# A decoder trunk's last layer: expert rows added to the output in DRAM instead of turned back into tokens

## Chip, cores and metric

The kernel runs on one core of a Trainium2 chip. The time is the device time of one execution in microseconds, as the median of the runs of a kernel. The engines are named as the profile names them: PE for matrix products (PEld is its weight load, which runs beside the products), DVE for vectors, ACT for activations, POOL for GpSimd, SP for the queue that starts most DMAs.

## The reference

A trunk of two layers over 256 tokens of width 1024, all in float32. Layer 0 is attention and a dense SwiGLU, layer 1 a gated recurrence and a layer of 8 experts, of which each token uses 2. Only the last part is touched here:

```python
logits = (t @ w_router).astype(F32)
top_vals, top_idx = lax.top_k(logits, TOP_K)
top_w = jax.nn.softmax(top_vals, axis=-1)
gates = jnp.sum(jax.nn.one_hot(top_idx, N_EXPERTS, dtype=F32) * top_w[..., None], axis=1)
out = jnp.zeros((B * S, D), F32)
for e in range(N_EXPERTS):
    y = swiglu(t, w_gate[e], w_up[e], w_down[e]).astype(F32)
    out = out + gates[:, e:e + 1] * y
```

The output is the residual `h` plus `out`. An expert's three matrices are 1024 x 3584, 1024 x 3584 and 3584 x 1024 floats, 44 MB together; all eight are read once, 352 MB.

## The kernel before

**Precision.** A product of float32 quality is made of three passes in a faster format: a weight is split into `w_hi` (ACT copies and rounds, L91) and `w_lo` (DVE subtracts, L91), rows likewise, and `mm3` (L100 to L103) issues high x high, high x low and low x high. A split covers 128 x 1024 weights and feeds six products of 128 x 128 by 512 columns. Split buffers are four deep (`NSUB`), buffers of raw weights fourteen deep (`NRAW`), 1 MB each; SP starts a load when a raw buffer comes free.

**Routing and slots.** `route` finds each token's two experts (`sel`), their weights (`gw`) and each token's slot in its expert's 128 rows (`place`, by products with a triangle of ones and a block of ones, L1034 to L1037). `one_hot` compares `place` with the slot numbers, and `gather_pair` multiplies the tokens' rows (`nh`, `nl`) by that 0/1 matrix: 32 products of 256 columns bring the rows of two experts into slots at once. Experts thus come in pairs: 0 and 1, 2 and 3, and so on.

**Jobs.** An expert's 3584 hidden columns are seven chunks of 512; a chunk is a `Job` with `gate`, `up`, `turn` (four transposes of the 128 x 512 hidden block, then `hh` on ACT and `hl` on DVE, one buffer each) and `down`, which accumulates in two banks `py` over all seven chunks. A job has twelve splits, that is 72 products, and reads 6.3 MB. `run_jobs` weaves them: gate of this job, turn of the one before, up, down of the one before. Before experts 2, 4 and 6 a job is `fresh`: the pair is gathered first, then the previous job is turned and finished. Which instruction really comes next on an engine's queue is settled at build time by the framework, which lets later work go ahead where it takes an engine for idle; the queue itself then runs strictly in order.

**Leaving the slots.** When an expert's last chunk is down, `back_to_tokens` transposes its two 0/1 blocks, and `scatter` takes `py` apart into a high and a low part (ACT and DVE, for each half of the columns), multiplies each by `back` (for two halves and two blocks of tokens, two products each: eight of 512 columns) and lets DVE add the result times the gate into `h` (L1204, four times). The last job does this half by half and sends `h` to the output with `put`, so the output is written once, at the very end.

**More than 128 tokens.** After all jobs a count of each expert's tokens is made (L1254 to L1261). Every engine loads the largest into a register and branches around a second pass that is needed only if some expert has more than 128 tokens. With these inputs it is skipped.

Of the kernel before, what the change touches and what calls it, by code (L numbers as in the profile page):

```python
# [39 lines left out]
def tile_trunk(  # L40
# [935 lines left out]
    mc = ctx.enter_context(tc.tile_pool(name="mc", bufs=1))  # L976

# [6 lines left out]
    _, _, rx, pw = norm_T(hg_, gain_m, acc, into=dense)  # L984

# [5 lines left out]
    nc.vector.tensor_scalar(ei, slot1[:, 0:NE], -1.0, None, op0=ALU.add)  # L991
    up = moe.tile([P, P], F32, name="up", tag="hm", bufs=1)
# [12 lines left out]
    sel = mc.tile([P, NT, NE], F32, name="sel")  # L1005
    gw = mc.tile([P, NT, NE], F32, name="gw")
    place = mc.tile([P, NT, NE], F32, name="place")

    def route():
# [10 lines left out]
        for t in range(NT):  # L1020
# [12 lines left out]

            pp = bank("tp")  # L1034
            for u in range(t + 1):
                nc.tensor.matmul(pp[:, 0:NE], lhsT=up if u == t else ones, rhs=sel[:, u], start=(u == 0), stop=(u == t))
            nc.vector.scalar_tensor_tensor(place[:, t], pp[:, 0:NE], 1.0, sel[:, t], op0=ALU.add, op1=ALU.mult)  # L1037
# [22 lines left out]
    def gather_pair(oneh):  # L1060
# [17 lines left out]
    NCH = FE // 512  # L1078

    class Job:  # L1080

        def __init__(self, ch, shared, es, weights, oneh, gates, fresh=None):
            self.ch, self.shared, self.es, self.oneh, self.gates, self.fresh = ch, shared, es, oneh, gates, fresh
# [39 lines left out]
        def down(self):  # L1123
# [10 lines left out]
            if ch == NCH - 1:  # L1134
                back = back_to_tokens(self.oneh(sh))
                for c in range(2):
                    scatter(c, sh["py"][c], back, self.gates(sh))

    class LastJob(Job):

        def down(self):
            sh = self.shared
            back = back_to_tokens(self.oneh(sh))
            for c in range(2):
# [5 lines left out]
                scatter(c, sh["py"][c], back, self.gates(sh), put)  # L1150

    class FirstJob(Job):
# [16 lines left out]
        def up(self):  # L1169
            sh = self.shared  # L1170
            sh["oneh"] = one_hot(0)
            sh["xg"] = gather_pair(sh["oneh"])
            pt = bank("tp")
# [8 lines left out]
    def back_to_tokens(oneh):  # L1182
        pt = bank("tp")
        for t in range(NT):
            nc.tensor.transpose(out=pt[:, t * P:(t + 1) * P], in_=f32(oneh[t]), identity=ident)
        back = moe.tile([P, S], F32R, name="back", tag="back", bufs=1)
        nc.scalar.activation(back, pt[:, 0:S], AF.Copy)
        return back

    def scatter(c, py, back, gate, done=None):  # L1190

        if c == 0:
            y = lows.tile([P, 2, 512], F32R, name="y", tag="low1")
            yh, yl = y[:, 0], y[:, 1]
        else:
            yh = moe.tile([P, 512], F32R, name="yh", tag="hh", bufs=1)
            yl = moe.tile([P, 512], F32R, name="yl", tag="hl", bufs=1)
        nc.scalar.activation(yh, py, AF.Copy)
        nc.vector.tensor_sub(yl, py, f32(yh))
        for t in range(NT):  # L1200
            ps = bank("tp")
            nc.tensor.matmul(ps, lhsT=back[:, TOK[t]], rhs=yh, start=True, stop=False)
            nc.tensor.matmul(ps, lhsT=back[:, TOK[t]], rhs=yl, start=False, stop=True)
            nc.vector.scalar_tensor_tensor(h[t][:, HALF[c]], ps, gate[t], h[t][:, HALF[c]], op0=ALU.mult, op1=ALU.add)  # L1204
            if done:
                done(t, c)
# [22 lines left out]
    for e in range(NE):  # L1229
        if e % 2 == 0:  # L1230
            shared = {}

            def fresh(sh, e=e):
                sh["oneh"] = one_hot(e)
                sh["xg"] = gather_pair(sh["oneh"])
# [4 lines left out]
        def oneh(sh, e=e):  # L1240
            return [sh["oneh"][:, t, e % 2, :] for t in range(NT)]

        def gates(sh, e=e):
            return [gw[:, t, e:e + 1] for t in range(NT)]

        for ch in range(NCH):
            kind = {(0, 0): FirstJob, (NE - 1, NCH - 1): LastJob}.get((e, ch), Job)
            jobs.append(kind(
                ch, shared, slice((e % 2) * P, (e % 2 + 1) * P), (moe_w_gate[0, e], moe_w_up[0, e], moe_w_down[0, e]), oneh, gates,
# [86 lines left out]
```

## Time and profile before

| what | value |
|---|---|
| median of 3 runs | 1505.01 us (1504.41 to 1505.1) |
| the profiled execution | 1505.47 us, its span 1503.8 us |
| TensorE clock granted, mean | 0.997 of full speed |
| PE, PEld busy | 98%, 82% |
| DVE, ACT, POOL busy | 83%, 69%, 1% |
| moved by DMA | 429.85 MB, 427.41 MB of it read from HBM |

The span runs from the first instruction to the last, and the execution takes some 1.7 us more around it. The layer of experts fills the span from about 490 us on. Matrix products are pipelined, so that the bars of two neighbours overlap: a busy PE tells that it has work, and the distance from one product's start to the next tells its pace.

### The profile page before, as it was taken

The numbers are of one execution on the slowest core, as the hardware profiler recorded it, in microseconds if no ns is written. First come the engines' busy times: TensorE is split into PE (matmuls) and PEld (weight loads), VectorE is DVE, ScalarE is ACT, GpSimd is POOL, SyncE is SP. The second block draws the span as 40 slices with busy tenths as digits, with TensorE's granted clock in tenths as the row PEclk, the third lists the DMA queues.
The fourth block names the chain that finished last, engine by engine and source line by source line (L and its number), as shares of the span: only waits on it lengthen the run. The fifth ranks groups of instructions, "written<-read, shape, count | busy, mean of one in ns | idle before, by whom it ended". The sixth has DMA issues, their size and how long they took to land.

```text
span 1503.8 us, 20241 instructions
## 1 busy us (share of the span) xinstructions
PE 1469.5 (98%) x7573; PEld 1226.1 (82%) x7573; DVE 1243.1 (83%) x1474; ACT 1042.0 (69%) x1293; POOL 14.9 (1%) x32
## 2 busy tenths in 40 slices
PE   7999999999999999999999999999999999999997
PEld 6886899998898788888888878888877888877885
DVE  7785655566777899999999998898889889889886
ACT  6655544445666788878778877777777777777774
POOL 1000000000000000000000000000000000000000
PEclk9999999999999999999999999999999999999999
DMA  9933455655454499999999999989999998999970
GB/s 310 368 122 112 152 175 193 187 180 180 141 168 141 159 369 376 373 357 378 326 340 385 368 339 359 358 325 362 358 365 345 370 357 319 363 362 346 365 253 31
DMA packets 208683, 429.85 MB, mean 286 GB/s; under 512 B 7290, under 2 KB 58530, under 8 KB 208578
## 3 DMA queue, kind: packets, MB, share of 16 engines
q1 hardware_dynamic: 208082, 426.82, 79.8%
q0 software_dynamic: 496, 1.67, 0.4%
q8 instruction: 61, 1.00, 0.3%
q14 instruction: 44, 0.36, 0.1%
HBM read 427.41 MB, written 1.05 MB: 285 GB/s over the span
## 4 chain that ended last, share of the span: by engine, by line
PE 91%; DVE 4%; ACT 2%; issue 1%; DMA 1%; POOL 0%; SPq 0%; ACTq 0%; DVEq 0%; POOLq 0%
PE acc L102 17%; PE acc L101 17%; PE acc L103 16%; PE pj L103 8%; PE pj L102 8%; PE pj L101 8%; PE pj L342 3%; PE pj L343 3%; PE pj L344 3%; DVE w_lo L91 2%; PE tp L1116 1%; PE pj L760 1%; PE pj L761 1%; PE pj L762 1%; ACT w_hi L91 1%
## 5 line engine op out<-in xcount | busy, mean ns | idle before, releaser
L91 DVE TENSOR_TENSOR w_lo<-raw,w_hi 128x1024 fp32r<-128x1024 f32 x810 | 958.5, 1221 | 155.0 <-ACT w_hi L91 137.8
L91 ACT ACTIVATE w_hi<-raw 128x1024 fp32r<-128x1024 f32 x810 | 835.9, 1058 | 271.1 <-PE acc L103 97.5
L102 PE MATMUL acc<-w_lo,xgh 128*128 128x512 f32 x904 | 357.1, 395 | 0.9
L101 PE MATMUL acc<-w_hi,xgh 128*128 128x512 f32 x904 | 355.8, 394 | 1.0 <-ACT xgh L294 1.0
L103 PE MATMUL acc<-w_hi,xgl 128*128 128x512 f32 x904 | 353.2, 391 | 0.0
L102 PEld LDWEIGHTS acc<-w_lo,xgh 128*128 128x128 f32 x904 | 169.7, 188 | 50.4 <-DVE w_lo L91 14.4
L101 PEld LDWEIGHTS acc<-w_hi,xgh 128*128 128x128 f32 x904 | 169.7, 188 | 36.3 <-ACT xgh L294 1.2
L103 PEld LDWEIGHTS acc<-w_hi,xgl 128*128 128x128 f32 x904 | 169.8, 188 | 33.9
L102 PE MATMUL pj<-w_lo,hh 128*128 128x512 f32 x448 | 177.1, 395 | 0.3
L103 PE MATMUL pj<-w_hi,hl 128*128 128x512 f32 x448 | 174.6, 391 | 0.3
L101 PE MATMUL pj<-w_hi,hh 128*128 128x512 f32 x448 | 161.1, 391 | 2.2 <-ACT hh L1120 1.7
L101 PEld LDWEIGHTS pj<-w_hi,hh 128*128 128x128 f32 x448 | 84.1, 188 | 21.5 <-ACT hh L1120 2.7
L102 PEld LDWEIGHTS pj<-w_lo,hh 128*128 128x128 f32 x448 | 84.2, 188 | 18.1 <-DVE w_lo L91 1.6
L103 PEld LDWEIGHTS pj<-w_hi,hl 128*128 128x128 f32 x448 | 84.0, 188 | 17.5 <-DVE hl L1121 1.1
L342 PE MATMUL pj<-xh,w_hi 128*128 128x256 f32 x320 | 90.8, 284 | 0.6 <-DVE hm L677 0.6
L343 PE MATMUL pj<-xl,w_hi 128*128 128x256 f32 x320 | 90.5, 283 | 0.0
L344 PE MATMUL pj<-xh,w_lo 128*128 128x256 f32 x320 | 90.5, 283 | 0.0
L1106 ACT ACTIVATE sg<-acc 128x512 f32<-128x512 f32 x55 | 33.0, 599 | 46.7 <-PE acc L103 46.7
L342 PEld LDWEIGHTS pj<-xh,w_hi 128*128 128x128 f32 x320 | 61.4, 192 | 1.2 <-DVE hm L677 0.8
L343 PEld LDWEIGHTS pj<-xl,w_hi 128*128 128x128 f32 x320 | 61.4, 192 | 0.4
L344 PEld LDWEIGHTS pj<-xh,w_lo 128*128 128x128 f32 x320 | 61.4, 192 | 0.0
L1120 ACT ACTIVATE hh<-tp 128x512 fp32r<-128x512 f32 x56 | 33.3, 595 | 40.4 <-PE pj L102 33.2
(296 smaller groups left out, 1637.1 us busy)
## 6 DMA issues: line engine op xcount, KB each, us to landing
raw<-in_moe_w_gate_dram SPq DMA_DIRECT2D x112, 1024.0 KB, 6.5
raw<-in_moe_w_up_dram SPq DMA_DIRECT2D x112, 1024.0 KB, 7.2
raw<-in_moe_w_down_dram SPq DMA_DIRECT2D x110, 1024.0 KB, 7.0
raw<-in_ffn_w_gate_dram SPq DMA_DIRECT2D x22, 512.0 KB, 3.8
raw<-in_ffn_w_up_dram SPq DMA_DIRECT2D x22, 512.0 KB, 4.8
raw<-in_ffn_w_down_dram SPq DMA_DIRECT2D x11, 1024.0 KB, 4.8
raw<-in_hgrn_w_in_dram SPq DMA_DIRECT2D x10, 1024.0 KB, 5.8
raw<-in_attn_w_in_dram SPq DMA_DIRECT2D x16, 512.0 KB, 9.3
```

What stands on the lines that cost most here:

```text
L91: split.last = nc.scalar.activation(hi, view, AF.Copy), nc.vector.tensor_sub(lo, view, f32(hi))
L101: nc.tensor.matmul(ps, lhsT=xh, rhs=wh, start=first, stop=False, skip_group_check=chk)
L102: nc.tensor.matmul(ps, lhsT=xh, rhs=wl, start=False, stop=False, skip_group_check=chk)
L103: nc.tensor.matmul(ps, lhsT=xl, rhs=wh, start=False, stop=last, skip_group_check=chk)
L342: nc.tensor.matmul(o, lhsT=wh[:, i, j], rhs=xh[:, k], start=k == 0 and j == 0, stop=False, skip_group_check=True)
L343: nc.tensor.matmul(o, lhsT=wh[:, i, j], rhs=xl[:, k], start=False, stop=False, skip_group_check=True)
L344: nc.tensor.matmul(o, lhsT=wl[:, i, j], rhs=xh[:, k], start=False, stop=k == KT - 1, skip_group_check=True)
L760: nc.tensor.matmul(o, lhsT=wh[:, k], rhs=xh[:, k], start=first, stop=False, skip_group_check=True)
L761: nc.tensor.matmul(o, lhsT=wh[:, k], rhs=xl[:, k], start=False, stop=False, skip_group_check=True)
L762: nc.tensor.matmul(o, lhsT=wl[:, k], rhs=xh[:, k], start=False, stop=last, skip_group_check=True)
L1106: nc.scalar.activation(self.sg, ps, AF.Silu)
L1120: nc.scalar.activation(self.hh, ptv, AF.Copy)
```

## The change

The residual `h` is written to the output before the experts start. From then on an expert's rows are added to the output in DRAM: ACT scales `py` by the slot's gate into a tile `y`, and POOL starts an indirect DMA that adds each of the 128 slot rows (4 KB) to the row of the output that an index names. `back_to_tokens` and `scatter` go. So that no slot is without a token, `place` is now a permutation of all 256 tokens for each expert, the chosen ones first, the others behind with a gate of 0. Token number and gate (in two parts) stand in `info`, and `slot_rows` brings them into slot order with four small products per pair.

The two scalings of an expert (`scaled`) wait in a list `later` and are placed on ACT behind the second and third split of the following gate. At a fresh pair the previous job's `turn` moves from behind the gather into its middle (`between`). The last job adds each half of the columns by its own DMA. The count now comes out of `route`. Small tiles get a pool `bits`.

```diff
+    for t in range(NT):
+        nc.gpsimd.dma_start(out=out[0, TOK[t], :], in_=h[t])
+    out_rows = out[0]
+    out_halves = out[0].rearrange("t (c d) -> (t c) d", c=2)
...
     def route():
...
-            pp = bank("tp")
-            for u in range(t + 1):
-                nc.tensor.matmul(pp[:, 0:NE], lhsT=up if u == t else ones, rhs=sel[:, u], start=(u == 0), stop=(u == t))
-            nc.vector.scalar_tensor_tensor(place[:, t], pp[:, 0:NE], 1.0, sel[:, t], op0=ALU.add, op1=ALU.mult)
...
+        pp = bank("tp")
+        for u in range(NT):
+            nc.tensor.matmul(pp[:, 0:NE], lhsT=ones, rhs=sel[:, u], start=(u == 0), stop=(u == NT - 1), skip_group_check=True)
+        for t in range(NT):
+            for u in range(t + 1):
+                nc.tensor.matmul(pp[:, (t + 1) * NE:(t + 2) * NE], lhsT=up if u == t else ones, rhs=sel[:, u], start=(u == 0),
+                                 stop=(u == t), skip_group_check=True)
+        nc.vector.tensor_copy(count, pp[:, 0:NE])
+        for t in range(NT):
+            before = pp[:, (t + 1) * NE:(t + 2) * NE]
+            u = bits.tile([P, 2, NE], F32, name="u", tag="u")
+            nc.vector.scalar_tensor_tensor(u[:, 0], before, 2.0, count, op0=ALU.mult, op1=ALU.subtract)
+            nc.vector.scalar_tensor_tensor(u[:, 0], u[:, 0], ntok[:, t:t + 1], sel[:, t], op0=ALU.add, op1=ALU.mult)
+            nc.vector.scalar_tensor_tensor(u[:, 1], before, -1.0, count, op0=ALU.mult, op1=ALU.add)
+            nc.vector.scalar_tensor_tensor(place[:, t], u[:, 1], tok[:, t:t + 1], u[:, 0], op0=ALU.add, op1=ALU.add)
+        nc.vector.tensor_scalar(place, place, 1.0, None, op0=ALU.add)
+        nc.vector.tensor_copy(info[:, :, :, 1], gw)
+        nc.vector.tensor_sub(info[:, :, :, 2], gw, f32(info[:, :, :, 1]))
...
+    def slot_rows(lhs, rhs, n):
+
+        ps = bank("tp")
+        for j in range(n):
+            for t in range(NT):
+                nc.tensor.matmul(ps[:, 4 * j:4 * j + 4], lhsT=lhs(t, j), rhs=rhs(t, j), start=(t == 0), stop=(t == NT - 1),
+                                 skip_group_check=True)
+        v = bits.tile([P, n, 4], F32, name="sv", tag=f"sv{n}")
+        nc.vector.tensor_copy(v, ps[:, 0:4 * n].rearrange("p (j c) -> p j c", c=4))
+        gate = bits.tile([P, n], F32, name="gate", tag=f"gate{n}")
+        nc.vector.tensor_add(gate, v[:, :, 1], v[:, :, 2])
+        idx = bits.tile([P, 3, n], I32, name="idx", tag=f"idx{n}")
+        nc.vector.tensor_copy(idx[:, 0], v[:, :, 0])
+        for c in range(2):
+            nc.vector.tensor_scalar(idx[:, 1 + c], v[:, :, 0], 2.0, float(c), op0=ALU.mult, op1=ALU.add)
+        return gate, idx
...
+    def gather_pair(oneh, between=None):
 
         xg = slot_tiles(2 * P)
         for k0 in range(0, KT, 2):
+            if k0 == 4 and between:
+                between()
...
     def into(self, w):
...
+                    if later and k0 + i:
+                        with tc.issue_after(split.last[0].ins):
+                            later.pop(0)()
...
     def down(self):
...
             if ch == NCH - 1:
-                back = back_to_tokens(self.oneh(sh))
-                for c in range(2):
-                    scatter(c, sh["py"][c], back, self.gates(sh))
+                later.extend(self.add(0, 2, out_rows, 0))
+
+        def add(self, c0, c1, rows, i):
+
+            (gate, idx), j, py = self.shared["slots"], self.slot, self.shared["py"]
+            box = {}
+
+            def scaled(c):
+                if c == c0:
+                    box["y"] = lows.tile([P, 2, 512], F32, name="y", tag="low1")
+                nc.scalar.activation(box["y"][:, c], py[c], AF.Copy, scale=gate[:, j:j + 1])
+                if c == c1 - 1:
+                    out_of(box["y"])
+
+            def out_of(y):
+                nc.gpsimd.indirect_dma_start(
+                    out=rows, out_offset=bass.IndirectOffsetOnAxis(ap=idx[:, i, j:j + 1], axis=0),
+                    in_=y[:, c0:c1].rearrange("p a b -> p (a b)"), in_offset=None, bounds_check=rows.shape[0] - 1,
+                    oob_is_err=True, compute_op=ALU.add)
+
+            return [lambda c=c: scaled(c) for c in range(c0, c1)]
 
     class LastJob(Job):
...
-            back = back_to_tokens(self.oneh(sh))
             for c in range(2):
...
-                scatter(c, sh["py"][c], back, self.gates(sh), put)
+                for step in self.add(c, c + 1, out_halves, 1 + c):
+                    step()
...
             if job and job.fresh:
-                job.fresh(job.shared)
-                if prev:
-                    prev.turn()
-                    prev.down()
-                    prev = None
+                job.fresh(job.shared, prev.turn)
+                prev.down()
+                prev = None
...
-    pc_ = bank("tp")
-    nc.tensor.matmul(pc_[:, 0:NE], lhsT=ones, rhs=sel[:, 0], start=True, stop=False)
-    nc.tensor.matmul(pc_[:, 0:NE], lhsT=ones, rhs=sel[:, 1], start=False, stop=True)
     cmax = mc.tile([P, 1], F32, name="cmax")
-    nc.vector.tensor_reduce(out=cmax, in_=pc_[:, 0:NE], axis=AX.X, op=ALU.max)
+    nc.vector.tensor_reduce(out=cmax, in_=count, axis=AX.X, op=ALU.max)
```

The second pass and its loop get the same treatment; it is not executed here.

## Rows read from the trace of the kernel before

**Rows 1.** The page: the chain that ended last, and the two groups of splits.

```profile
PE 91%; DVE 4%; ACT 2%; issue 1%; DMA 1%; POOL 0%; SPq 0%; ACTq 0%; DVEq 0%; POOLq 0%
...
L91 DVE TENSOR_TENSOR w_lo<-raw,w_hi 128x1024 fp32r<-128x1024 f32 x810 | 958.5, 1221 | 155.0 <-ACT w_hi L91 137.8
L91 ACT ACTIVATE w_hi<-raw 128x1024 fp32r<-128x1024 f32 x810 | 835.9, 1058 | 271.1 <-PE acc L103 97.5
```

**Rows 2.** Waits from 620 to 1480 us: waiter, releaser, total us, times, longest.

```profile
ACT w_hi L91 <- PE acc L103: 45.1, 151, 1.2
...
PEld acc L102 <- DVE w_lo L91: 14.4, 36, 0.6
```

**Rows 3.** Waits of SP's queue over the span, same columns.

```profile
SPq L85 <- DVE w_lo L91: 1173.8, 381, 17.2
```

**Rows 4.** Windows, 550 to 600 us: engines' busy us, clock, DMA share, GB/s.

```profile
550.00:600.00 50.00, 50.00 (x228) 41.40 (x227) 46.45 (x42) 40.73 (x42) 0.00 (x0) 1.00 1.01 376
```

**Rows 5.** DMA issues: count, KB each, median us to landing.

```profile
raw<-in_moe_w_gate_dram SPq DMA_DIRECT2D x112, 1024.0 KB, 6.5
...
out_dram<-h SPq DMA_DIRECT2D x4, 256.0 KB, 2.1
```

**Rows 6.** Timeline of ACT: the gates' activations, and two of `hh`.

```profile
523.14 0.60 ACT L1106 ACTIVATE sg<-acc 128x512 f32<-128x512 f32 x1 [0.31 <-PE acc L103]
...
623.99 0.60 ACT L1106 ACTIVATE sg<-acc 128x512 f32<-128x512 f32 x1 [0.30 <-PE acc L103]
624.49 0.59 ACT L1120 ACTIVATE hh<-tp 128x512 fp32r<-128x512 f32 x1
...
643.06 0.60 ACT L1106 ACTIVATE sg<-acc 128x512 f32<-128x512 f32 x1 [0.31 <-PE acc L103]
...
659.83 0.60 ACT L1106 ACTIVATE sg<-acc 128x512 f32<-128x512 f32 x1 [0.30 <-PE acc L103]
...
727.04 0.60 ACT L1106 ACTIVATE sg<-acc 128x512 f32<-128x512 f32 x1 [0.30 <-PE acc L103]
...
767.47 0.60 ACT L1106 ACTIVATE sg<-acc 128x512 f32<-128x512 f32 x1 [0.30 <-PE acc L103]
...
1310.59 0.60 ACT L1120 ACTIVATE hh<-tp 128x512 fp32r<-128x512 f32 x1 [1.45 <-PE pj L102]
...
1333.38 0.60 ACT L1106 ACTIVATE sg<-acc 128x512 f32<-128x512 f32 x1 [1.30 <-PE acc L103]
...
1350.50 0.60 ACT L1106 ACTIVATE sg<-acc 128x512 f32<-128x512 f32 x1 [1.30 <-PE acc L103]
...
1422.54 0.60 ACT L1106 ACTIVATE sg<-acc 128x512 f32<-128x512 f32 x1 [1.31 <-PE acc L103]
...
1473.84 0.60 ACT L1106 ACTIVATE sg<-acc 128x512 f32<-128x512 f32 x1 [1.30 <-PE acc L103]
```

**Rows 7.** Timeline of PE at the change from expert 1 to 2.

```profile
743.32 0.50 PE L101 MATMUL pj<-w_hi,hh 128*128 128x512 f32 x1 [0.47 <-ACT hh L1120]
```

**Rows 8.** The end: timeline from 1484 us, and line 1262's branch on PE.

```profile
1489.93 0.60 ACT L1198 ACTIVATE y<-pj 128x512 fp32r<-128x512 f32 x1 [1.93 <-PE pj L103]
...
1493.03 0.39 PE L103 MATMUL pj<-w_hi,hl 128*128 128x512 f32 x1
...
L1262 PEldq COMPARE_BRANCH  x1: 4448/4448/4448, 1498.2 to 1498.2; - x1
```

**Rows 9.** Timelines of POOL, DVE and PE at the start of the experts.

```profile
488.73 0.96 POOL L997 DMA_DIRECT2D gT<-in_moe_w_router_dram  x1
...
488.85 0.69 DVE L310 TENSOR_TENSOR hg<-h,gain 128x512 f32<-128x512 f32 x1
...
491.33 0.68 DVE L310 TENSOR_TENSOR hg<-h,gain 128x512 f32<-128x512 f32 x1
...
504.90 0.17 DVE L1037 SCALAR_TENSOR_TENSOR place<-tp,sel 128x8 f32<-128x8 f32 x1 [0.69 <-PE tp L1036]
...
506.42 0.63 PE L1069 MATMUL acc<-oneh,nh 128*128 128x256 f32 x4
```

More of the change, by code (lines that the diff above doesn't have):

```diff
@@ L976, in tile_trunk @@
     mc = ctx.enter_context(tc.tile_pool(name="mc", bufs=1))
+    bits = ctx.enter_context(tc.tile_pool(name="bits", bufs=2))
     def slot_tiles(n):
@@ L991, in tile_trunk @@
     nc.vector.tensor_scalar(ei, slot1[:, 0:NE], -1.0, None, op0=ALU.add)
+    ti = bits.tile([P, NT], I32, name="ti", tag="ti", bufs=1)
+    nc.gpsimd.iota(ti, pattern=[[P, NT]], base=0, channel_multiplier=1)
+    tok = mc.tile([P, NT], F32, name="tok")
+    nc.vector.tensor_copy(tok, ti)
+    ntok = mc.tile([P, NT], F32, name="ntok")
+    nc.vector.tensor_scalar(ntok, tok, -1.0, None, op0=ALU.mult)
     up = moe.tile([P, P], F32, name="up", tag="hm", bufs=1)
@@ L1005, in tile_trunk @@
     sel = mc.tile([P, NT, NE], F32, name="sel")
+    zero = mc.tile([P, NT * NE], F32, name="zero")
+    nc.gpsimd.memset(zero, 0.0)
     gw = mc.tile([P, NT, NE], F32, name="gw")
     place = mc.tile([P, NT, NE], F32, name="place")
+    count = mc.tile([P, NE], F32, name="count")
+    info = mc.tile([P, NT, NE, 4], F32R, name="info")
+    nc.vector.tensor_copy(info[:, :, :, 3], zero[:, 0:NT * NE].rearrange("p (t e) -> p t e", e=NE))
+    nc.vector.tensor_copy(info[:, :, :, 0], tok[:, :, None].to_broadcast([P, NT, NE]))
     def route():
@@ L1058, in one_hot, with pair_rows @@
         return oneh
-    def gather_pair(oneh):
+    def slot_rows(lhs, rhs, n):
[13 more added lines that the diff above has]
+        return gate, idx
+    def pair_rows(oneh, e):
+        return slot_rows(lambda t, j: oneh[:, t, j], lambda t, j: info[:, t, e + j], 2)
+    def gather_pair(oneh, between=None):
         xg = slot_tiles(2 * P)
         for k0 in range(0, KT, 2):
+            if k0 == 4 and between:
+                between()
             for src, dst in ((nh, xg[0]), (nl, xg[1])):
@@ L1078, in tile_trunk, with __init__ @@
     NCH = FE // 512
+    later = []
     class Job:
-        def __init__(self, ch, shared, es, weights, oneh, gates, fresh=None):
-            self.ch, self.shared, self.es, self.oneh, self.gates, self.fresh = ch, shared, es, oneh, gates, fresh
+        def __init__(self, ch, shared, es, weights, slot, fresh=None):
+            self.ch, self.shared, self.es, self.slot, self.fresh = ch, shared, es, slot, fresh
             self.wg, self.wu = [w.rearrange("(kt p) c -> p kt c", p=P) for w in weights[:2]]
@@ L1172, in up @@
             sh["xg"] = gather_pair(sh["oneh"])
+            sh["slots"] = pair_rows(sh["oneh"], 0)
             pt = bank("tp")
@@ L1180, in up @@
             super().up()
[L1182 to L1206, printed above, removed]
     def run_jobs(jobs):
@@ L1231, in tile_trunk, with fresh @@
             shared = {}
-            def fresh(sh, e=e):
+            def fresh(sh, between, e=e):
                 sh["oneh"] = one_hot(e)
-                sh["xg"] = gather_pair(sh["oneh"])
+                sh["xg"] = gather_pair(sh["oneh"], between)
+                sh["slots"] = pair_rows(sh["oneh"], e)
             if e == 0:
                 route()
[L1240 to L1244, printed above, removed]
         for ch in range(NCH):
@@ L1248, in tile_trunk @@
             jobs.append(kind(
-                ch, shared, slice((e % 2) * P, (e % 2 + 1) * P), (moe_w_gate[0, e], moe_w_up[0, e], moe_w_down[0, e]), oneh, gates,
+                ch, shared, slice((e % 2) * P, (e % 2 + 1) * P), (moe_w_gate[0, e], moe_w_up[0, e], moe_w_down[0, e]), e % 2,
                 fresh if e in (2, 4, 6) and ch == 0 else None))
     run_jobs(jobs)
-    pc_ = bank("tp")
-    nc.tensor.matmul(pc_[:, 0:NE], lhsT=ones, rhs=sel[:, 0], start=True, stop=False)
-    nc.tensor.matmul(pc_[:, 0:NE], lhsT=ones, rhs=sel[:, 1], start=False, stop=True)
     cmax = mc.tile([P, 1], F32, name="cmax")
-    nc.vector.tensor_reduce(out=cmax, in_=pc_[:, 0:NE], axis=AX.X, op=ALU.max)
+    nc.vector.tensor_reduce(out=cmax, in_=count, axis=AX.X, op=ALU.max)
     cmax_i = mc.tile([P, 1], I32, name="cmax_i")
@@ L1269, in tile_trunk @@
             pc = small.tile([P, NT, 2], F32, name="pc", tag="pc")
+            info2 = bits.tile([P, NT, 4], F32R, name="info2", tag="info2")
             oh2 = moe.tile([P, NT, P], F32R, name="oh2", tag="oneh")
@@ L1275, in tile_trunk @@
                 nc.vector.tensor_scalar(oh2[:, t], slot1, pc[:, t, 0:1], None, op0=ALU.is_equal)
+            nc.vector.tensor_copy(info2[:, :, 0], tok)
+            nc.vector.tensor_copy(info2[:, :, 1], pc[:, :, 1])
+            nc.vector.tensor_sub(info2[:, :, 2], pc[:, :, 1], f32(info2[:, :, 1]))
+            nc.vector.tensor_copy(info2[:, :, 3], zero[:, 0:NT])
             xg2 = slot_tiles(P)
@@ L1286, in tile_trunk @@
             ws = [w[0, bass.ds(e, 1)].rearrange("o a b -> (o a) b") for w in (moe_w_gate, moe_w_up, moe_w_down)]
-            shared = dict(xg=xg2)
-            run_jobs([Job(ch, shared, slice(0, P), ws,
-                          lambda sh: [oh2[:, t] for t in range(NT)], lambda sh: [pc[:, t, 1:2] for t in range(NT)])
-                      for ch in range(NCH)])
+            shared = dict(xg=xg2, slots=slot_rows(lambda t, j: oh2[:, t], lambda t, j: info2[:, t], 1))
+            run_jobs([Job(ch, shared, slice(0, P), ws, 0) for ch in range(NCH)])
+            while later:
+                later.pop(0)()
             nc.vector.tensor_scalar(ecur, ecur, 1.0, None, op0=ALU.add)
-        dump()
 _INS = ['x', 'attn_norm', 'attn_w_in', 'attn_w_out', 'ffn_norm', 'ffn_w_gate', 'ffn_w_up', 'ffn_w_down',
```

## The prediction

> **What bounds the kernel now.** I read the page first, then the waits, then the time from gate to gate on ACT, then the end.
>
> The chain is PE work for 91% [rows 1]. From 620 us on, ACT waits for PE to release split buffers (45.1 us in 151 waits for `acc` alone), while PE waits little for splits [rows 2]: in the experts PE sets the pace, and the splits run ahead of it as far as four buffers allow.
>
> DMA looks like a second bound: share 1.01 at 376 GB/s [rows 4]. The other two views speak against it. SP waits 1173.8 us for DVE to free raw buffers [rows 3], and a 1 MB load lands 6.5 us after its issue [rows 5]. At 376 GB/s that is 2.4 MB under way, out of fourteen buffers of 1 MB: the other eleven or so hold weights that wait for PE.
>
> The gates' activations on ACT are a clock for the jobs [rows 6]. An early job takes 659.83 - 643.06 = 16.77 us, and 72 products in that are at most 0.233 us each. A late one takes 1350.50 - 1333.38 = 17.12 us for the same products. The difference is an order of instructions. In the early jobs `hh` stands right behind `sg` and waits for nothing; in the late ones ACT meets it earlier and stands 1.45 us until PE is done with the old `hh`, then 1.30 us before `sg`. The next splits come late, and PE waits for `w_lo`, 14.4 us in all [rows 2]. I call these the quick and the slow order. By the same clock some 22 of the later jobs are slow, and after each gather two jobs are quick again.
>
> From the first gate shown to the last are 54 steps: 1473.84 - 523.14 = 950.7 us, against 54 x 16.77 = 905.6 us of pure quick jobs. The 45.1 us above that hold all the boundaries between experts and the slow order; they are what the change can reach there.
>
> **Part by part.**
>
> *Scatter inside a pair (experts 0-1, 2-3, 4-5, 6-7).* It removes eight products of 512 columns, 8 x 0.23 = 1.84 us of PE, and two transposes, about 0.2: 2.04 us. The first such boundary costs 19.07 - 16.77 = 2.3 us [rows 6], so little more than its PE work. The late ones cost more: from 1350.50 to 1422.54 are four steps, 72.04 us, against 4 x 17.12 = 68.48, so 3.6 us; the other two late ones read alike. The surplus is DVE's: a split takes 1.22 us on it [rows 1], twelve of them 14.6 us of a 17 us job, and the scatter adds six operations on 512 columns. Both PE's and DVE's part go. What replaces them is two scalings on ACT, which did two copies of the same size before and also `back`. They stand behind splits of a gate, where ACT waits for PE anyway; were that cover gone, they would cost at most 2 x 0.6 us per expert. I take -2.3 - 3 x 3.6 = -13.1 us; if only PE's own work goes, -8.2.
>
> *Gather boundaries (three).* 767.47 - 727.04 = 40.43 us for two steps, 6.9 above two quick jobs [rows 6]. The gather itself, 32 products of half the width, is 3.7 of it, the scatter 2.04. The first `down` product waits 0.47 us for `hh` [rows 7], because `turn` and `down` follow each other; with `turn` in the middle of the gather, sixteen products (1.9 us) cover the copy and that wait goes. The four small products of `slot_rows` are not in this trace: their cost lies between nothing and four full products, 0.9 us; I take half. Per boundary -2.04 - 0.5 + 0.45 = -2.1, so -6.3 us; bounds -7.6 and -3.4.
>
> *The order.* What brings the slow order back is time: it sets in after some twenty jobs, and each boundary, with its additional PE work, buys a few quick jobs. With the inner boundaries shrunk to nothing they buy none, and the slow order should set in earlier. I take eight more slow jobs at 0.33: +2.6 us. Bounds: no slow jobs, -7.3; all others slow too, +10.6.
>
> *The start.* `place` is now made after both blocks are routed, with some ten small DVE operations and two copies for `info` ahead of `one_hot`. The old chain is done at 504.90 and the gather starts at 506.42 [rows 9]; a small operation is about 0.1 to 0.17 us, so that much slack is about used up. I take +1 us, between 0 and 2.5. The two writes of `h` stand ahead of the router's load on POOL at about 1 us each [rows 9]; PE has the dense gate to do meanwhile, and the raw buffers are full: nothing.
>
> *Adds and weight loads.* Seven adds of 512 KB, read and written, 7 MB beside 340 MB of weights. At 376 GB/s that is 2.8 us each, in front of eleven full buffers worth some 30 us: nothing. An add would have to hold all DMA engines for about 30 us before PE starved. On POOL's queue nothing stands behind an add but the next add, some 118 us later, and nobody waits for it until `y` is used again.
>
> *The end.* Now `py`'s first half is read at 1489.93 and PE's last `down` product starts at 1493.03; then come scatter, count and PE's branch, which alone takes 4.45 us from 1498.2 [rows 8] and ends the kernel about 1 us later. Afterwards the count is long known, and PE, without the first half's scatter, is done by about 1492.2. But the two halves use one buffer `y`: the second scaling waits until the first add has landed, and POOL's second add follows that. A leg is a scaling (0.6), POOL's issue (0.96 for the router's load [rows 9]) and a landing, which the trace doesn't show for an add: below, 2.1 us as for a plain write [rows 5]; above, 6.5 as for a load amid others. I take 3.5, nearer to the write, since the queues are empty by then: legs from 1489.7 to 1494.8 and to 1499.8. If PE loads the count only when ACT and POOL have issued, its branch ends near 1502. I take -2 us, between -5 and +6.5.
>
> *POOL beside DVE.* The add reads its row numbers from SBUF while DVE works on `w_lo`, from two SBUF tiles, most of the time. In this trace, POOL's issue of 0.96 us at 488.73 lies over a DVE product of two SBUF tiles that takes 0.69 us; the same product without it takes 0.68 [rows 9]. So nothing, with a bound among the rivals. The Trainium skill, "SBUF — State Buffer", section "Who interferes with whom", speaks against the change here: a DVE instruction with two SBUF inputs and a GpSimd instruction that reads SBUF exclude each other for a whole instruction. The row doesn't show it, but its load isn't an indirect one, so the rule is not refuted. By the rule alone DVE would stand still for each add's time on POOL.
>
> **The sum.** -13.1 - 6.3 + 2.6 + 1 - 2 = -17.8 us. From the profiled execution's 1505.5 that is 1487.7; the median of the runs is 0.5 lower, so 1487 us.
>
> **The rivals.**
>
> *Quick order throughout.* For it: less DVE work at the boundaries, which is where the disorder starts. Against it: the order was lost in spite of quick boundaries before. -13.1 - 6.3 - 7.3 + 1 - 2 = -27.7: 1477 us. Chance 0.15.
>
> *The order takes it back.* All jobs after the first gather slow, and only PE's own work gone from the boundaries: -8.2 - 3.4 + 10.6 + 1 - 2 = -2: 1503 us. For it: the clock of rows 6 shows boundaries as the only thing that mends the order. Chance 0.15.
>
> *The end gets longer.* Two adds in a row at the upper landing: -17.8 + 8.5 = -9.3: 1496 us. Chance 0.1.
>
> *DVE stands still for the adds (the other side).* For it: `w_lo` runs some 85% of the time, and every add falls into a gate. Against it: the 0.69 beside the 0.68. Its price: a split buffer becomes free about three splits, 4.1 us, before PE wants it full; copy and subtraction take 2.3 [rows 1], so some 2 us of standing still are free. Beyond that PE loses what DVE loses. Seven adds of 6 us cost 7 x (6 - 2) = 28 us: 1515. It decides from 17.8 / 7 + 2 = 4.5 us per add on. Chance 0.1.
>
> **How the numbers follow.** The forecast has 0.5, with a range of its own from 1482 to 1493 by the smaller bounds. From 1476 to 1502 lie the forecast, the first and the third rival, and about half of the second; outside are the other half and the last, some 2 in 10. This kernel's runs differ so little that 0.2%, 3 us, is about what can be told from no change. Faster by more: 0.5 + 0.15 + 0.1 + 0.06 = 0.81. Within it: 0.06, of the second rival. Slower: 0.03 of it and 0.1, so 0.13.
>
> **What will show it.** Gate to gate: the steps over inner boundaries as long as their neighbours, those over a gather about 4.7 us above two jobs. ACT's waits before `hh` and `sg` count the slow jobs; if their number is far from 30, the third term is wrong. `w_lo` near an add: if one of them starts late with POOL as the releaser, or takes well over 1.2 us, the last rival holds. At the end, the time from the first add's issue to its landing, and what PE's branch waits for. If PE's pace between boundaries changes, which I hold fixed at 16.77 or 17.12, the forecast is wrong at its base.

## The result and the profile after

| kernel | median of runs | range |
|---|---|---|
| before | 1505.05 us (4 runs) | 1504.41 to 1506.45 |
| after | 1488.32 us (4 runs) | 1487.72 to 1489.99 |

The ratio is 0.9882, with a 95% interval of 0.9867 to 0.9897: 16.7 us faster; 1487 us was forecast. The profiled execution of after is the longest of its four (1489.99 us, span 1488.3 us).

The page of after, busy shares and the two groups of splits, beside [rows 1]:

```profile
PE 1453.3 (98%) x7509; PEld 1216.6 (82%) x7509; DVE 1213.9 (82%) x1460; ACT 1035.2 (70%) x1285; POOL 31.9 (2%) x45
...
L91 DVE TENSOR_TENSOR w_lo<-raw,w_hi 128x1024 fp32r<-128x1024 f32 x810 | 956.8, 1221 | 169.2 <-ACT w_hi L91 153.5
L91 ACT ACTIVATE w_hi<-raw 128x1024 fp32r<-128x1024 f32 x810 | 830.0, 1057 | 248.4 <-PE acc L103 82.9
```

A split costs what it did, 1221 and 1057 ns. PE has as large a share as before, of a span that is 15.5 us shorter.

The gates' activations on ACT, after: the step over the first inner boundary, the first gather, and one late inner boundary. They answer to [rows 6].

```profile
627.92 0.60 ACT L1163 ACTIVATE sg<-acc 128x512 f32<-128x512 f32 x1 [0.30 <-PE acc L103]
...
644.71 0.60 ACT L1163 ACTIVATE sg<-acc 128x512 f32<-128x512 f32 x1 [0.30 <-PE acc L103]
...
728.74 0.60 ACT L1163 ACTIVATE sg<-acc 128x512 f32<-128x512 f32 x1 [0.30 <-PE acc L103]
...
766.60 0.60 ACT L1163 ACTIVATE sg<-acc 128x512 f32<-128x512 f32 x1 [0.30 <-PE acc L103]
...
1339.09 0.60 ACT L1163 ACTIVATE sg<-acc 128x512 f32<-128x512 f32 x1 [1.30 <-PE acc L103]
...
1356.21 0.60 ACT L1163 ACTIVATE sg<-acc 128x512 f32<-128x512 f32 x1 [1.30 <-PE acc L103]
...
1373.58 0.60 ACT L1163 ACTIVATE sg<-acc 128x512 f32<-128x512 f32 x1 [0.91 <-PE acc L103]
```

The first inner boundary is gone: 644.71 - 627.92 = 16.79 us, as long as the jobs beside it. The late one takes 1373.58 - 1356.21 = 17.37 beside 17.12: 0.25 left of 3.6. The first gather takes 766.60 - 728.74 = 37.86 for two steps where it took 40.43. From the first gate (527.08) to the last (1459.09) are 932.0 us, against 950.7: **18.7 us less**. With a first gate that comes 3.9 us later and an end that is 0.8 us shorter (both below), that makes up the 15.5 us between the two profiled spans.

Waits of after from 620 to 1480 us, as [rows 2] (waiter, releaser, total us, times, longest):

```profile
ACT sg L1163 <- PE acc L103: 50.9, 49, 1.7
...
ACT hh L1177 <- PE pj L102: 43.4, 30, 1.5
ACT w_hi L91 <- PE acc L103: 30.5, 104, 0.3
...
PEld acc L102 <- DVE w_lo L91: 14.6, 41, 0.4
```

The slow order is still there, and longer: 30 waits of `hh` where before had 22. The first slow step ends at 851.39, where it ended at 923.28 before, and no gather mends the order any more: 32 steps are slow jobs.

The end, timeline of ACT and POOL, beside [rows 8]:

```profile
1474.91 0.69 ACT L1202 ACTIVATE y<-pj,gate 128x512 f32<-128x512 f32 x1 [1.92 <-PE pj L103]
1475.88 1.54 POOL L1207 DMA_INDIRECT out_dram<-y,idx  x1 [103.94 <-ACT y L1202]
1480.86 0.69 ACT L1202 ACTIVATE y<-pj,gate 128x512 f32<-128x512 f32 x1 [5.26 <-DMA out_dram<-y,idx]
1481.82 1.54 POOL L1207 DMA_INDIRECT out_dram<-y,idx  x1 [4.40 <-ACT y L1202]
```

The second scaling waits 5.26 us for the first add, as forecast; a leg from scaling to scaling is 1480.86 - 1474.91 = 5.95 us. From the last gate to the end are 29.2 us, 0.8 less than before.

The start, timeline of DVE and PE, beside [rows 9]:

```profile
507.49 0.17 DVE L1065 COPY count<-tp 128x8 f32<-128x8 f32 x1 [1.10 <-PE tp L1063]
...
510.01 0.17 DVE L1073 TENSOR_SCALAR place<-place 128x16 f32<-128x16 f32 x1
510.22 1.43 DVE L1087 TENSOR_TENSOR oneh<-slot,place 128x256 fp32r<-128x256 f32 x4
...
510.70 0.39 PE L1122 MATMUL acc<-oneh,nh 128*128 128x256 f32 x1 [1.30 <-DVE oneh L1087]
```

From the copy of the count to the last operation on `place` are 2.7 us of DVE, a split of 1.22 among them, and PE stands 1.30 us for `oneh`. From DVE's additions that finish `h` (at 488.06 us) to the first gate are 39.0 us where there were 37.5 (from 485.64). Another 2.4 us of difference lie ahead of that, in instructions that both kernels have; two kernels below that differ from after only behind the first gate have the same 39.0 us, but the additions at 486.05 (a_oneadd) and at 491.17 (a_noadd), so I count the 2.4 us to no part of the change.

An add beside DVE, timeline of POOL and DVE:

```profile
640.41 1.69 POOL L1207 DMA_INDIRECT out_dram<-y,idx  x1 [144.11 <-DVE w_lo L91]
641.10 4.63 DVE L91 TENSOR_TENSOR w_lo<-raw,w_hi 128x1024 fp32r<-128x1024 f32 x4 [0.88 <-ACT w_hi L91]
```

Four `w_lo` in a row take 4.63 us, and the first lies for 1.0 us beside the add's 1.69 us on POOL; the idle time before it is put down to ACT.

### The profile page after: what moved, and what is told of

The parts are those of the page before. It is cut to its first block, busy times and chain, and to the rows that moved or that the text cites. A ratio compares the mean times of both kernels' runs of the same rounds, so it can differ in the third digit from the quotient of the medians.

```text
span 1488.3 us, 20143 instructions
## 1 busy us (share of the span) xinstructions
PE 1453.3 (98%) x7509; PEld 1216.6 (82%) x7509; DVE 1213.9 (82%) x1460; ACT 1035.2 (70%) x1285; POOL 31.9 (2%) x45
## 3 DMA queue, kind: packets, MB, share of 16 engines
HBM read 427.41 MB, written 5.24 MB: 291 GB/s over the span
## 4 chain that ended last, share of the span: by engine, by line
issue 53%; PE 37%; DMA 5%; DVE 2%; ACT 2%; POOL 0%; SPq 0%; POOLq 0%; ACTq 0%; DVEq 0%
PE acc L101 5%; PE acc L102 5%; PE acc L103 5%; DMA out_dram<-y,idx 4%; PE pj L342 3%; PE pj L344 3%; PE pj L343 3%; PE pj L101 2%; PE pj L103 2%; PE pj L102 2%; DVE w_lo L91 1%; PE pj L760 1%; PE pj L761 1%; PE pj L762 1%; PE tp L556 1%
## 5 line engine op out<-in xcount | busy, mean ns | idle before, releaser
L91 DVE TENSOR_TENSOR w_lo<-raw,w_hi 128x1024 fp32r<-128x1024 f32 x810 | 956.8, 1221 | 169.2 <-ACT w_hi L91 153.5
L91 ACT ACTIVATE w_hi<-raw 128x1024 fp32r<-128x1024 f32 x810 | 830.0, 1057 | 248.4 <-PE acc L103 82.9
L102 PEld LDWEIGHTS acc<-w_lo,xgh 128*128 128x128 f32 x904 | 169.6, 188 | 51.8 <-DVE w_lo L91 14.6
L101 PE MATMUL pj<-w_hi,hh 128*128 128x512 f32 x448 | 158.1, 391 | 0.7 <-ACT hh L1177 0.5
```

Source lines behind the costliest of these rows:

```text
L91: split.last = nc.scalar.activation(hi, view, AF.Copy), nc.vector.tensor_sub(lo, view, f32(hi))
L101: nc.tensor.matmul(ps, lhsT=xh, rhs=wh, start=first, stop=False, skip_group_check=chk)
L102: nc.tensor.matmul(ps, lhsT=xh, rhs=wl, start=False, stop=False, skip_group_check=chk)
```

## Experiments

Each kernel was timed in five rounds beside the kernel before on the same chip, whose medians there were 1505.4 to 1505.7 us (1505.05 beside after). "Gate to gate" is from the first `sg` to the last, 932.0 us in after and 950.7 in before.

**Holding the transposes back (a_pin, b_pin).** The 30 waits of `hh` suggested that the transposes are issued too early.

```diff
-            if prev:
+            if prev and job:
+                with tc.issue_after(mm3.last.ins):
+                    prev.turn()
+            elif prev:
                 prev.turn()
```

> The changed kernel, with the four transposes of turn held on PE behind the last product of the next job's gate, so that they can no longer go ahead into the down products. My theory is that the slow order of the later jobs (17.1 us a job, 32 of them in the changed kernel) comes from those early transposes alone: all jobs then take 16.8 us, ACT's waits before hh for PE (43.4 us) go, and the kernel gains 32 x 0.33 = 10.6 us: some 1478 us. Rival 1: the slow order comes from splits that lag for another reason, and holding the transposes back only moves the wait: 1487 to 1490 us. Rival 2: holding them opens a new hole on PE at each job, behind the gate: slower than 1490 us.

> The kernel before, with the same hold on the transposes of turn. By my theory its 22 slow jobs become quick (-7.3 us) and the late scatter boundaries cost as much as the first one, 2.3 instead of 3.6 us (-4 us): some 1494 us; what is then left between this and the held changed kernel, some 16 us, is the work of the scatter itself. Rival: the late boundaries' surplus is DVE's own load and stays: 1498 us. If the order has nothing to do with the transposes: 1505 us.

Measured: 1501.16 us (1499.61 to 1503.4), ratio 0.9967 [0.9956, 0.9979], and 1515.13 (1513.98 to 1516.94), ratio 1.006 [1.0045, 1.0074]. Both are slower than without the hold: my theory fell. A late job of a_pin, timeline of ACT, DVE and PEld:

```profile
1297.11 0.60 ACT L1163 ACTIVATE sg<-acc 128x512 f32<-128x512 f32 x1 [1.66 <-PE acc L103]
1297.60 0.59 ACT L1177 ACTIVATE hh<-tp 128x512 fp32r<-128x512 f32 x1
1298.08 4.90 ACT L91 ACTIVATE w_hi<-raw 128x1024 fp32r<-128x1024 f32 x5
...
1299.17 3.50 DVE L91 TENSOR_TENSOR w_lo<-raw,w_hi 128x1024 fp32r<-128x1024 f32 x3 [0.26 <-ACT w_hi L91]
1300.45 0.19 PEld L102 LDWEIGHTS acc<-w_lo,xgh 128*128 128x128 f32 x1 [0.37 <-DVE w_lo L91]
```

`hh` waits for nothing now, and yet the late jobs take 17.49 us instead of 17.1. What waits is `sg`, 1.66 us, and behind it `hh` and five splits in a row. That leaves the place of `sg`. A quick and a slow job of after, ACT's timeline (of the slow one DVE's and PEld's too):

```profile
626.55 1.06 ACT L91 ACTIVATE w_hi<-raw 128x1024 fp32r<-128x1024 f32 x1 [0.30 <-PE acc L103]
627.92 0.60 ACT L1163 ACTIVATE sg<-acc 128x512 f32<-128x512 f32 x1 [0.30 <-PE acc L103]
...
1302.53 1.05 ACT L91 ACTIVATE w_hi<-raw 128x1024 fp32r<-128x1024 f32 x1
1304.87 0.60 ACT L1163 ACTIVATE sg<-acc 128x512 f32<-128x512 f32 x1 [1.30 <-PE acc L103]
1305.37 4.91 ACT L91 ACTIVATE w_hi<-raw 128x1024 fp32r<-128x1024 f32 x5
...
1306.45 3.50 DVE L91 TENSOR_TENSOR w_lo<-raw,w_hi 128x1024 fp32r<-128x1024 f32 x3 [1.05 <-ACT w_hi L91]
...
1307.73 0.19 PEld L102 LDWEIGHTS acc<-w_lo,xgh 128*128 128x128 f32 x1 [0.37 <-DVE w_lo L91]
```

In the quick job `sg` stands behind a split (`up`'s third) and its 0.30 us of waiting is what any split has there. In the slow one it stands ahead of that split: ACT waits 1.30 us for the gate's last product, the split comes late, DVE waits 1.05 us for it and PE 0.37 for DVE.

**Holding `sg` behind `up`'s third split (a_hold, b_hold, a_sg).** The activation moves out of `gate` into `up`; a_hold and b_hold hold `turn` there too, a_sg holds `sg` alone.

```diff
-            ps, = self.into(self.wg)
+            self.pg, = self.into(self.wg)
...
+                    if mid and k0 + i == 4:
+                        with tc.issue_after(split.last[0].ins):
+                            mid()
...
+            def mid():
+                self.silu()
+                if turn:
+                    with tc.issue_after(self.gated.ins):
+                        turn()
+            ps, = self.into(self.wu, mid)
```

> The changed kernel, with sg and hh on ACT held behind up's third split of every job, as the early jobs have them, and hh's transposes behind the gate's last product on PE. My theory now: the late jobs are slow because sg stands on ACT ahead of up's third split, so that this split's two halves come late; where the transposes stand is only a consequence. Then all jobs keep some 16.8 us from gate to gate and the 32 slow ones give back 0.33 us each: 1488.3 - 10.6, about 1478 us. Rival: the order of sg and the third split is a consequence of something else too; then the late jobs stay at 17.1 us or above and the time is 1488 or, if sg held back makes hh late for the next down, up to 1500.

> The same hold in the kernel before. By my theory its 22 slow jobs give back 0.33 us each, 7.3 us, and its three late inner boundaries shrink from 3.6 us towards the first one's 2.3, another 4: about 1494 to 1498 us. If so, the distance from the changed kernel with the same hold is what the parts of the change are worth without the order: some 16 to 18 us. Rival, as above: 1505 us or more.

> The changed kernel with sg alone held behind up's third split; turn (the transposes, hh, hl) stands where the change has it. If the place of sg alone makes the jobs slow, the late jobs take 16.8 us and the time is that of the kernel with both held, about 1480 us. If the place of hh makes them slow too, ahead of the third split with its wait of some 1.45 us for PE's last reader of the old hh, the late jobs stay at 17.1 us or between, and the time is 1484 to 1489 us.

Measured: a_hold 1479.94 us (1479.2 to 1482.69), ratio 0.9831 [0.9818, 0.9845]; a_sg 1480.23 (1479.04 to 1484.53), ratio 0.9838 [0.9822, 0.9855]; b_hold 1499.94 (1499.28 to 1501.98), ratio 0.9964 [0.995, 0.9977]. First a late job of a_sg, ACT's timeline, and then two of its waits from 620 to 1470 us:

```profile
1290.87 0.60 ACT L1185 ACTIVATE hh<-tp 128x512 fp32r<-128x512 f32 x1 [1.43 <-PE pj L102]
1291.37 4.90 ACT L91 ACTIVATE w_hi<-raw 128x1024 fp32r<-128x1024 f32 x5
1296.56 0.60 ACT L1169 ACTIVATE sg<-acc 128x512 f32<-128x512 f32 x1 [0.29 <-PE acc L103]
```

```profile
ACT hh L1185 <- PE pj L102: 43.3, 30, 1.5
...
PEld acc L102 <- DVE w_lo L91: 2.2, 8, 0.3
```

This decides it. `hh` still waits 30 times, 43.3 us in all, and costs nothing: late jobs take 16.83 us (16.81 in a_hold), and PE's wait for `w_lo` falls from 14.6 to 2.2 us. The place of `sg` alone makes a job slow. Of the 10.6 us expected, 8.4 came, in the medians and gate to gate (923.6 us in a_hold): the steps behind the three late inner boundaries still take some 17.25 us, as does one other, and the late gathers 0.6 to 0.7 more than the first.

In the kernel before, the same hold gives 5.7 us, and its late jobs go to 16.8 too; but its late inner boundaries do not shrink towards 2.3 us, as I had expected. Three steps over one take 54.56 us, 4.1 above three quick jobs. With `sg` held in both, the change is worth 1499.94 - 1479.94 = 20.0 us.

**The scatter's two halves (a_hold_pe, a_hold_dve).** Each gives one engine's work back to a_hold, as work that nobody reads. PE's stands in one block behind the last `down` product, DVE's behind the two scalings; neither waits for the other engine, as the two do in the scatter itself.

```diff
+                pt = bank("tp")
+                for t in range(NT):
+                    nc.tensor.transpose(out=pt[:, t * P:(t + 1) * P], in_=f32(self.hh[:, t]), identity=ident)
+                for _ in range(4):
+                    ps = bank("tp")
+                    for k in range(2):
+                        nc.tensor.matmul(ps, lhsT=self.hh[:, k], rhs=self.hh.rearrange("p a b -> p (a b)"), start=k == 0, stop=k == 1)
                 later.extend(self.add(0, 2, out_rows, 0))
```

```diff
                 nc.scalar.activation(box["y"][:, c], py[c], AF.Copy, scale=gate[:, j:j + 1])
+                if rows is out_rows:
+                    nc.vector.tensor_sub(h[0][:, HALF[c]], py[c], box["y"][:, c])
+                    for t in range(NT):
+                        nc.vector.scalar_tensor_tensor(h[t][:, HALF[c]], py[c], gate[:, j:j + 1], h[t][:, HALF[c]],
+                                                       op0=ALU.mult, op1=ALU.add)
```

> The changed kernel with sg held, and, at the end of each of experts 0 to 6, only the scatter's work on PE given back: eight products of 512 columns and two transposes into banks that nobody reads. My prediction has 2.04 us of PE for these, 7 times: 1479.9 + 14.3, about 1494 us. Rival: the scatter's price lay elsewhere, in its waits, and bare products fit into gaps of PE; then well under 1490 us.

> The changed kernel with sg held, and only the scatter's work on DVE given back behind each scaling of experts 0 to 6: six operations on 512 columns per expert, written over the old h, which nobody reads any more. The prediction says that DVE's part costs nothing at the first inner boundary and 1.3 us at each of the three late ones, so some 4 to 6 us: about 1484 to 1486 us. Rival: DVE has room for them beside splits that run ahead; then 1480 us and the late boundaries' surplus in the kernel before came of the way in which PE and DVE wait for each other.

Measured: a_hold_pe 1494.08 us (1492.59 to 1497.95), ratio 0.9927 [0.991, 0.9944], as expected; a_hold_dve 1496.71 (1492.62 to 1498.71), ratio 0.994 [0.9924, 0.9955], some three times the expected cost. Five of its six runs had a mean granted clock of 0.993 to 0.995 where the profiled one has 0.996 and 1492.62 us, so I go by gate to gate of the profiled ones, in us above three quick steps of 16.81 for inner boundaries and two for the first gather (the first inner one over two steps):

| kernel | gate to gate | first inner | late inner | first gather |
|---|---|---|---|---|
| a_hold | 923.6 | 0.0 | 0.5 | 4.3 |
| a_hold_pe | 936.8 | 2.1 | 2.5 | 6.4 |
| a_hold_dve | 936.5 | 1.8 | 2.4 | 6.0 |
| b_hold | 945.9 | 2.2 | 4.1 | 6.8 |

Either engine's part alone costs 13 us over the seven boundaries; b_hold stands 22 above a_hold, of which the turn's old place at the gathers is some 1.5 to 3.7 (see the next experiment). At the first inner boundary they overlap and cost no more than one; at the late ones they nearly add up. The late boundary of a_hold_dve, timeline of DVE and PE's weight loads:

```profile
1126.09 1.41 DVE L1217 SCALAR_TENSOR_TENSOR h<-pj,gate,h 128x512 f32<-128x512 f32 x2
...
1128.69 0.19 PEld L102 LDWEIGHTS acc<-w_lo,xgh 128*128 128x128 f32 x1 [1.10 <-DVE w_lo L91]
...
1130.29 1.40 DVE L1217 SCALAR_TENSOR_TENSOR h<-pj,gate,h 128x512 f32<-128x512 f32 x2
...
1132.87 0.19 PEld L102 LDWEIGHTS acc<-w_lo,xgh 128*128 128x128 f32 x1 [0.83 <-DVE w_lo L91]
```

DVE has 12 x 1.22 us of splits in a job and two operations of 0.69 (`hl`, `hm`), 16.0 of 16.8 us. Six more of about 0.7 make 20.2, more than a quick job has, so here DVE runs out without any of PE's products.

At the first boundary the six stand otherwise than in the scatter. Timeline of DVE, a_hold_dve with PE's weight load, then b_hold with one product of PE:

```profile
638.05 1.28 DVE L1215 TENSOR_TENSOR h<-pj,y 128x512 f32<-128x512 f32 x2
639.25 2.72 DVE L1217 SCALAR_TENSOR_TENSOR h<-pj,gate,h 128x512 f32<-128x512 f32 x4
...
643.15 0.19 PEld L102 LDWEIGHTS acc<-w_lo,xgh 128*128 128x128 f32 x1 [1.90 <-DVE w_lo L91]
```

```profile
637.11 1.41 DVE L1218 SCALAR_TENSOR_TENSOR h<-tp,gw,h 128x512 f32<-128x512 f32 x2
638.44 1.22 DVE L91 TENSOR_TENSOR w_lo<-raw,w_hi 128x1024 fp32r<-128x1024 f32 x1
639.57 1.40 DVE L1218 SCALAR_TENSOR_TENSOR h<-tp,gw,h 128x512 f32<-128x512 f32 x2
640.89 1.22 DVE L91 TENSOR_TENSOR w_lo<-raw,w_hi 128x1024 fp32r<-128x1024 f32 x1
...
642.61 0.39 PE L102 MATMUL acc<-w_lo,xgh 128*128 128x512 f32 x1
```

In a_hold_dve all six run in a row with no split between, and PE waits 1.90 us behind them; in b_hold a split goes between, and PE waits for no `w_lo` there. So the 1.8 us hold for the place that they have in a_hold_dve. For the scatter's own order there is an estimate: b_hold's last split shown is done at 642.11, 0.50 us before PE takes it, and with 2.04 us of products less PE would have wanted it 1.5 us before it was done.

Why both parts add up late only, one row of b_hold suggests (timeline of ACT, first and a late inner boundary):

```profile
635.44 0.39 ACT L1201 ACTIVATE back<-tp 128x256 fp32r<-128x256 f32 x1
...
1119.61 0.39 ACT L1201 ACTIVATE back<-tp 128x256 fp32r<-128x256 f32 x1 [1.45 <-PE tp L1199]
1119.89 4.89 ACT L91 ACTIVATE w_hi<-raw 128x1024 fp32r<-128x1024 f32 x5
```

Late, `back` stands ahead of five splits and waits 1.45 us, which would use up the splits' lead before the scatter begins; at 871 us `hh`, just ahead of `back`, waits 1.66 us in the same place. That the lead is gone can be seen on PE's weight loads, 5.8 us ahead of the scatter's first (at 1128.03); at the first boundary no such wait stands ahead of the scatter:

```profile
1122.25 0.19 PEld L102 LDWEIGHTS pj<-w_lo,hh 128*128 128x128 f32 x1 [0.35 <-DVE w_lo L91]
```

That the place of `back` is what takes it is argued, not shown.

**The turn amid the gather (a_turnback, b_turnamid).**

```diff
-                job.fresh(job.shared, prev.turn)
+                job.fresh(job.shared, None)
+                prev.turn()
```

(b_turnamid does the opposite in the kernel before.)

> The changed kernel with one part undone: at the gathers, turn stands behind the gather again instead of amid it. By my prediction each of the three boundaries then waits about 0.47 us for hh again: 1488.3 + 1.4, about 1490 us. Rival: the wait was hidden anyway or the surplus of a gather has another cause; then 1488 us. A larger change, up or down, would be the order's.

> The kernel before with one part of the change alone: turn amid the gather, the scatter as it was. By my prediction three waits of 0.47 us go: 1505.0 - 1.4, about 1503.6 us, which is hardly more than the runs differ. Rival: nothing; a larger difference would be the order's.

Measured: a_turnback 1492.01 us (1490.96 to 1493.16), ratio 0.9906 [0.9891, 0.9922]; b_turnamid 1504.21 (1503.09 to 1506.4), ratio 0.9993 [0.9984, 1.0002]. In the changed kernel the part is worth 3.7 us (3.6 gate to gate) and not 1.4: the first gather's two steps take 38.81 us without it, 0.95 more, and around a late one four steps take 1.15 more. In the kernel before it is worth 1.5 us by the medians, which the interval can't tell from nothing; its first gather's steps become 0.68 us shorter.

**The adds among the experts (a_noadd).** This kernel leaves the adds of experts 0 to 6 out; only the last expert's rows reach the output.

```diff
-                if c == c1 - 1:
+                if c == c1 - 1 and c1 - c0 == 1:
                     out_of(box["y"])
```

> The changed kernel without the adds of experts 0 to 6 (their rows are scaled but not added; only the last job's two adds remain). It measures what seven adds cost. By my theory nothing: the same as the changed kernel within 1 us, 1488 us. Rival 1: the adds hold up weight loads or DVE, so that without them the kernel is faster by 2 us or more. Rival 2: the last add's landing waits for earlier ones, faster by less than 1 us.

Measured: 1488.99 us (1487.72 to 1493.17), ratio 0.9886 [0.9869, 0.9902], the same as after. From gate to gate both have 932.0 us. Seven adds cost nothing that can be measured. Timeline of DVE at the place of the first add, now without it:

```profile
644.18 4.63 DVE L91 TENSOR_TENSOR w_lo<-raw,w_hi 128x1024 fp32r<-128x1024 f32 x4 [0.88 <-ACT w_hi L91]
```

The same 4.63 us for four, and the same 0.88 us of idle time before them: neither was the add's.

**One add at the end, and the two gains together (a_oneadd, a_hold_oneadd).**

```diff
-                for step in self.add(c, c + 1, out_halves, 1 + c):
-                    step()
+                steps = self.add(0, 2, out_rows, 0) if c == 0 else steps
+                steps[c]()
```

> The changed kernel, with one add of 4 KB rows for the last job in place of two adds of 2 KB rows; the two scalings stay where they were and share one tile. By my theory the end of the changed kernel is the chain scaling, add, landing, scaling, add, landing; with one add the second scaling no longer waits 5.3 us for the first add's landing. It is done at about 1478.1 in the changed kernel's time, POOL starts 0.3 us later, the add lands 5 to 6.5 us after that, and the kernel ends 1.3 us on: 1.9 to 3.4 us earlier, some 1485.5 us. Rival: the landing grows with the bytes and takes back what the wait gave, no change.

> The changed kernel with sg held and with one add at the end in place of two. The two gains lie at different places, the experts and the end, so they should add up: 1479.9 - 2.3, about 1477.6 us. Rival: they share a wait, then 1479.9 us.

Measured: a_oneadd 1486.03 us (1485.85 to 1486.8), ratio 0.9867 [0.9849, 0.9885]; a_hold_oneadd 1477.74 (1476.62 to 1482.7), ratio 0.9817 [0.9798, 0.9836], the fastest of all. In both the second scaling waits for PE alone, and the single add of a_oneadd is issued at 1476.31 (its first gate is at 525.02), where the second add of after is issued at 1481.82 (first gate 527.08).

## Why the prediction was right, and where not

Its steps against gate to gate and the two ends of the profiled executions. Quick jobs are 16.805 us long (728.74 - 527.08 over twelve steps); the 16.77 that I took was the step behind a boundary, which is a little short. Over 54 steps before is 43.2 us above quick jobs, after 24.5.

| term | forecast | measured |
|---|---|---|
| inner boundaries | -13.1 | -12.3 (0.8 left in three late ones) |
| gathers | -6.3 | -7.5 (20.2 above the jobs around them before, 12.7 after) |
| order | +2.6 | +1.1 (the rest: 10.0 before, 11.1 after) |
| start | +1 | +1.5 |
| end | -2 | -0.8 |
| sum | -17.8 | -18.0 |

The jobs around a late gather are a slow and a quick one before, and two slow ones after. Gathers and order can't be parted sharply: measured against quick jobs alone, the gathers give 6.9 us and the order costs 0.5. The 2.4 us ahead of the experts stand in no term, and with them the profiled spans differ by 15.5 us. The terms miss by +0.8, -1.2, -1.5, +0.5 and +1.2 us, and that these nearly cancel is luck.

**Inner boundaries.** Right to 0.8 us. That DVE's part goes too was right, and the lower bound, PE's part alone, would have been far off. But my account of it was too kind to DVE: I let its six operations cost nothing at the first boundary, because the first boundary cost PE's 2.3 us. In a_hold_dve they cost 1.8 there by themselves, and by the estimate from b_hold's rows some 1.5 in the scatter's own order: they were hidden behind PE's products, which were about as long. Had the change removed PE's products alone, DVE would have kept more than half of the price, as far as a_hold_dve stands for it: the four inner boundaries cost 1.8 + 3 x 2.4 = 9.0 us there, against 2.2 + 3 x 4.1 = 14.5 in b_hold and 1.5 in a_hold.

**Gathers.** The mechanism was right, the size of the turn's part too small: I took the 0.47 us of one visible wait, and it measured 0.95 to 1.15, the later ones with steps before and after the gather that are longer too. The rest came as forecast: without the turn's part the first gather's steps take 40.43 - 38.81 = 1.62 us less than before, and 2.04 - 0.45 = 1.59 was taken for the scatter less `slot_rows`, which no run measures apart.

**Order.** 30 slow jobs were forecast, 32 came, but the mechanism was wrong. I held boundaries to be what mends the order, and counted `hh`'s wait into its cause. a_sg keeps `hh`'s waits and has quick jobs. What makes a job slow is that `sg` stands ahead of `up`'s third split on ACT's queue. So the first rival's quick order was not a matter of luck: it can be asked for, and a_hold gets within 3 us of that rival's 1477. Why the framework puts `sg` there from 833.82 us on, earlier than in the kernel before, stays open.

**Adds, weight loads, POOL beside DVE.** All nothing, by a_noadd; loads land 0.6 to 0.9 us later than before by the page's medians (7.4 us for a gate's 1 MB against the 6.5 of [rows 5]), most of it without the adds too (7.1 in a_noadd), and nobody waits for them. I counted seven adds as 7 MB read and written; for all eight experts the page has 4.2 MB more written to HBM than before (5.24 against 1.05) and the same 427.41 MB read. The Trainium skill's rule, "SBUF — State Buffer", section "Who interferes with whom", was taken in the prediction to make DVE stand still for each add's time on POOL; that use of it is not borne out: the rows above show `w_lo` as long, and as late, beside an indirect add as without one, and its mean over the kernel is the same 1221 ns.

**Start and end.** Both as described and both 0.5 to 1.2 us dearer than taken. The end's leg is 5.95 us where I took 5.06 (0.6, 0.96 and 3.5): POOL's issue of an add takes 1.54 us and not 0.96, and some 0.3 us lie between scaling and issue. It stayed inside the bounds, so the rival with the longer end did not come.

## What to carry to other kernels

When two engines are each nearly full beside each other, a boundary's price that equals one engine's work says nothing about the other's: remove both, or measure each alone, before one of them is called free. ACT took its instructions here strictly as they were queued: it stood 1.30 us before `sg` with five splits behind it that then ran without a wait. So an instruction that waits for the last product of a stage should stand behind the work that could already run; look at what is queued behind a waiting instruction before counting the wait as the cost. Of several waits that come and go together, hold one at a time: here the 30 waits of `hh`, 43 us in all, cost nothing, and the place of `sg` beside it cost 8.

## What the runs showed of the hardware

An indirect add of 128 rows from SBUF takes POOL 1.54 to 1.83 us to issue (nine in after), and lands 6.5 us after its issue in the median; the one at the idle end released its tile 4.98 us after issue. One add of whole rows in place of two of half rows spares the end the wait for the first (5.26 us in after), and 2.3 us of the time. And executions of one kernel with a mean granted clock of 0.993 or 0.994 of 2.4 GHz were 4 to 6 us longer than those with 0.996 or 0.997 (a_hold_dve 1498.71 at 0.993 and 1492.62 at 0.996, a_noadd 1493.17 at 0.994 and 1487.72 at 0.997), as much as several of the effects studied here: that is why the steps between gates decided, where medians lay close.
